# A two-layer trunk: value products of attention in one run, and a last norm applied to token rows

## The chip, the cores and the metric

One NeuronCore of one Trainium2 chip runs the whole kernel. The metric is device microseconds of one execution. Five engines work side by side, each through its own instructions in a fixed order: TensorE (PE; its weight loads are listed as PEld), VectorE (DVE), ScalarE (ACT), GpSimd (POOL) and SyncE (SP, which here only issues DMAs). TensorE reads SBUF and writes PSUM, which has eight banks of 512 fp32 per partition; VectorE and ScalarE read and write both.

## The reference

Two layers over 256 tokens of width 1024, everything in float32. Layer 0 mixes tokens by multi-scale pooling, layer 1 by attention over shared keys and values; each mixer is followed by a causal convolution FFN (inner width 2816) and a gated per-layer embedding, and the whole ends in an RMS norm. What the change touches, cut to its core:

```python
def rmsnorm(x, g):
    return x * lax.rsqrt(jnp.mean(x * x, axis=-1, keepdims=True) + EPS) * g

# attention, 16 heads of 64 in 4 groups; three branches, each a softmax over its keys
o_c = einsum('bghqc,bgcd->bghqd', p_c, vc)          # 15 compressed keys
o_s = einsum('bghqk,bgqkd->bghqd', p_s, vs_g)       # selected blocks
o_w = einsum('bghqk,bgkd->bghqd', p_w, vw)          # window of 512
out = gate0 * o_c + gate1 * o_s + gate2 * o_w

return rmsnorm(x, norm_final)                       # (1, 256, 1024)
```

With 256 tokens the selected blocks and the window are both all causal keys.

## The kernel before, in words

The residual stream `x` lies channel-major in SBUF: 8 tiles (KT) of 128 channels by 256 tokens. A large product is made of three TensorE products of fp32r parts (high times high, high times low, low times high); the parts of weights and activations are split off by ScalarE and VectorE.

**Attention.** Heads are taken two at a time; there are 8 such pairs (`pairs`), numbered n, and the order is written out by hand in `LOOP` (L50): one word is one step, `+1` and `+2` are steps for a later pair, `X` is a slice of filler work (the compressed branch, later the output projection). For a pair the steps are S (scores on PE), M (row maxima, DVE), E (exponentials with sums, ACT), F (factors), W (weighting of the probabilities), T (`turn`: four PE transposes of 128x128 into one PSUM bank, three times, z = 0, 1, 2), P (`parts`: copy of such a bank to SBUF, tile `pt`; z = 0 on ACT, z = 1 and 2 on DVE), V (`values`) and G (`gather`). The written order is not the final one: a planner issues, for each engine, the instruction of highest priority that it takes for ready; the priority is the place in the program, moved forward or back by the entries of `PR` (L60, `lead`).

`values(n, u, z)` (L833) works for two pairs at once, so only for odd n. It multiplies turned probabilities (128 keys by 512 columns) with values (128 keys by 64) into one bank `o`: pair n - 1 (s = 0) goes to PSUM partitions 0 to 63, pair n (s = 1) to 64 to 127, so that each product uses 64 of the 128 columns of the array. z = 0 and 1 are one product of 512 columns per pair, z = 2 is two of 256 columns per pair, z = 3 is the compressed branch (512 columns, tiles `vz` and `pc`). They are fp32, and each product shows as two weight loads and two matmuls in the profile. The order is s = 0, then s = 1 in each z. `V0` and `V1` stand in the middle of the round, `V2` and `V3` near its end, and `V3` has a priority of -20. All have the line of the helper `mm`, L99. `gather` (L900) reads bank `o` when all of it is there (ACT L907, DVE L908) and makes the operand `xo` of the output projection, which is filler work from n = 5 on and, for its last part, follows the loop (`tail`, L957).

**Last norm (L990 to L1016).** For each of the 8 tiles of `x`: ACT squares it (L1001), POOL adds tiles 0 to 5 (L1003), and ACT multiplies the tile by its gain (`scaled`, L996) into `xg`. One-column products on PE sum over partitions: the sum of tiles 0 to 5 first, then tile 6, then the two halves of tile 7. `rstd_of` (DVE L216, POOL L218) makes the factor r per token, with tokens on partitions. As `xg` has its tokens along the free dimension, `row_of` (L257) spreads r to all partitions: two diagonal matrices (DVE L264, ACT L262) and two products with ones. VectorE multiplies `xg` with that row in four steps of 128x512 (L1015), and each step is sent out by a DMA of 256 KB (L1016), from SP and ACT in turn. The host transposes the result.

Of the kernel before, what the change touches and what calls it, by code (L numbers as in the profile page):

```python
# [10 lines left out]
F32 = mybir.dt.float32  # L11
# [3 lines left out]
AF = mybir.ActivationFunctionType  # L15
ALU = mybir.AluOpType
AX = mybir.AxisListType

P = 128
T = 256  # L20
D = 1024
KT = D // P
# [22 lines left out]
BANKS = ((1, 2, 3), (0, 4))  # L45
# [1 line left out]
LEAD = 2  # L47


LOOP = 'W2 S0+2 X S2+1 X W0 X T0 M1+1 T1 M2+1 P0 E2+1 X X X T2 E1+1 P1 V0 M0+2 V1 P2 S1+2 X F+1 E0+2 X W1+1 V2 V3 G X X'  # L50

FILL = (('c0', -2), ('c1', 3), ('o0', 5), ('o1', 7))

# [3 lines left out]

PTS = 8

PR = {'P1': 100, 'W0': 40, 'W2': 100, 'V3': -20, 'w': -20, 'M1': 10}  # L60

PRE = 1

# [15 lines left out]
def body(ctx, tc, xt, xT, pT, pos, colsd, band, wpool, wup, wdn, wgate, wproj, wkv, wq, wqg, wout,  # L79
         cw1, cw2, out):  # L80
    nc = tc.nc
    V, S, E, G = nc.vector, nc.scalar, nc.tensor, nc.gpsimd
    const = ctx.enter_context(tc.tile_pool(name="const", bufs=1))
    wp = ctx.enter_context(tc.tile_pool(name="wp", bufs=3))
    xp = ctx.enter_context(tc.tile_pool(name="xp", bufs=2))
# [4 lines left out]
    def lead(what):  # L90

        n = PR.get(what, 0)
        return tc.high_priority(offset=n) if n else ExitStack()

    def bank(i, shape=(P, 2, T), dt=F32):
        return psum.tile(list(shape), dt, name=f"bank{i}", tag=f"bank{i}")

    def mm(o, w, x, first, last):
        E.matmul(o, w, x, start=first, stop=last, skip_group_check=True)  # L99
# [15 lines left out]
    for layer in range(2):  # L115
        if layer:
            chunks += [(wkv[k], 1) for k in range(KT)]
            n = len(chunks)
# [33 lines left out]
    def take():  # L152
        ahead(1)
        taken[0] += 1
        w = made[taken[0] - 1]
        made[taken[0] - 1] = None
        return w
# [34 lines left out]
    def col(name, i=0, n=1):  # L192
        a = COLS[name][0] + i
        return cols[:, a:a + n]

    ident = col("ident", 0, 128)
# [16 lines left out]
    def rstd_of(ss, name):  # L213
        n = ss.shape[-1]
        m = sm.tile([P, n], F32, name="ms", tag="ms")
        V.tensor_scalar(m, ss, 1.0 / D, EPS, op0=ALU.mult, op1=ALU.add)  # L216
        r = sm.tile([P, n], F32, name=name, tag=name)
        G.tensor_tensor(r, m, mhalf[:, :n], op=ALU.pow)  # L218
        return r
# [13 lines left out]
    b = bank(7, (P, 512))  # L233
# [5 lines left out]
    for i in range(2):  # L239
        ss = sm.tile([P, 1], F32, name=f"ss{i}")  # L240
        S.activation(sqs, xtok[:, i], AF.Square, accum_out=ss)
        r = rstd_of(ss, f"rc{i}")
# [11 lines left out]
        else:  # L254
            S.activation(us[:, k], ub[k], AF.Copy, scale=col("mix0", k))

    def row_of(b, r, both=False):  # L257

        dg = xp.tile([P, 2, P], F32, name="dg", tag="sq", bufs=2)
        for i in range(2):  # L260
            if i and both:
                S.activation(dg[:, i], ident, AF.Copy, scale=r[:, i:i + 1])  # L262
            else:
                V.tensor_scalar(dg[:, i], ident, r[:, i:i + 1], None, op0=ALU.mult)  # L264
        for i in range(2):
            mm(b[:, 256 + i * P:256 + (i + 1) * P], ones, dg[:, i], True, True)
        return b[:, 256:]
# [257 lines left out]
    def attention_layer(ap):  # L525
# [6 lines left out]
        for i in range(2):  # L532
            t = ap.tile([P, 2048], F32, name="w1", tag="big", bufs=2)
            nc.sync.dma_start(t, cw1[i])
            w1.append(t.rearrange("p (i h) -> p i h", i=16))
            t = ap.tile([P, 64], F32, name=f"w2{i}", bufs=1)
# [11 lines left out]
        for k in range(KT):  # L548
            if k == KT - 1:
                rows = finish()  # L550
            w = take()
# [8 lines left out]
        rc, row = rows()  # L560
# [11 lines left out]
        def rope(src, n, w, cc, sc_):  # L572
            sh = ap.tile([P, 512], F32, name="rsh", tag="rsh", bufs=2)
            t = ap.tile([P, 512], F32, name="rt", tag="rt", bufs=1)
            v = lambda a: a[:, :n * w].rearrange("p (n w) -> p n w", n=n)
            if n * w == 512:
                V.stream_shuffle(v(sh), src, SHUF)
            else:
                S.copy(v(t), src)
                V.stream_shuffle(sh[:, :n * w], t[:, :n * w], SHUF)  # L580
            bc = lambda a: a[:, None, :].to_broadcast([P, n, w])
            V.tensor_tensor(v(t), src, bc(cc), op=ALU.mult)
            V.tensor_tensor(v(sh), v(sh), bc(sc_), op=ALU.mult)
            V.tensor_add(t[:, :n * w], t[:, :n * w], sh[:, :n * w])
            return v(t)
# [25 lines left out]
        VV = ap.tile([P, 2, 8, 64], F32, name="vv", bufs=1)  # L611
# [48 lines left out]
        for i in range(2):  # L660
            hb = bank((7, 1)[i], (P, 512))
            o = hb[:, 0:75]
# [6 lines left out]
            h = ap.tile([P, 60], F32, name="gh", tag="gh", bufs=1)  # L669
            V.tensor_scalar(h, o[:, 0:60], bcol, None, op0=ALU.add)  # L670
            t = ap.tile([P, 60], F32, name="gt", tag="gtt", bufs=1)
# [7 lines left out]
            if i == 0:  # L679
                for s in range(2):  # L680
                    mm(hb[s * 64:(s + 1) * 64, 256:286].rearrange("p (a b) -> p a b", a=2), w2[0],
                       gl[:, s::2, :], True, True)
                t = rope(hb[:, 256:286].rearrange("p (a b) -> p a b", a=2), 2, 15, Cc_[:, 0, 0:15],
                         Cc_[:, 1, 0:15])
# [3 lines left out]
            else:  # L688
# [6 lines left out]
                for p in range(2):  # L695
                    o = hb[:, 256 + p * 64:320 + p * 64]
# [3 lines left out]
                VZ = ap.tile([P, 4, 2, 64], F32, name="vz", bufs=1)  # L700
                G.memset(VZ, 0.0)
                for j in range(4):
                    k = slice(32 * j, 32 * j + 32)
# [126 lines left out]
            else:  # L830
                S.copy(t, u["t", z])

        def values(n, u, z):  # L833


            p, s, jj = pairs[n]
            if not s:
                return
            if z == 0:
                u["o"] = bank(BANKS[1][n // 2 % len(BANKS[1])], (P, 512))  # L840
            for t in range(2 if z == 2 else 1):
                for s in range(2):
                    g = 2 * p + s
                    w = U[n - 1 + s]["h", z] if z < 3 else PC[p]
                    v = VV[:, 0, 4 * z + g] if z < 2 else VV[:, 1, 4 * t + g] if z == 2 else VZ[:, 2 * jj + s, p]
                    o = u["o"][64 * s:64 * s + 64]
                    if z == 2:
                        o, w = o[:, T:], w[:, t * T:(t + 1) * T]
                    mm(o, v, w, z == 0, z == 3)


        PC = {}
# [71 lines left out]
        U = {}  # L924
# [18 lines left out]
        for n in range(-LEAD, NPAIR):  # L943
# [6 lines left out]
            if n in FLUSH:  # L950
                filler(100)
            for w in LOOP.split():
                step(w, n)
# [36 lines left out]
    b = bank(2, (P, 512))  # L990
    acc = xp.tile([P, T], F32, name="sqa", tag="sqa", bufs=1)
    xg = xp.tile([P, 2, KT, T], F32, name="xg", tag="xs", bufs=2)
    xg, sq = xg[:, 0], xg[:, 1]

    def scaled(k):
        S.activation(xg[:, k], x[:, k], AF.Copy, scale=col("final", k))  # L996

    for k in range(KT):
        for i in range(2 if k == KT - 1 else 1):
            c = slice(i * P, i * P + P) if k == KT - 1 else slice(0, T)  # L1000
            S.activation((acc if k == 0 else sq[:, k])[:, c], x[:, k, c], AF.Square)  # L1001
        if 0 < k < KT - 2:
            G.tensor_tensor(acc, acc, sq[:, k], op=ALU.add)  # L1003
        if k >= KT - 3:
            for i in range(2):
                mm(b[:, i:i + 1], (acc if k == KT - 3 else sq[:, k])[:, i * P:(i + 1) * P], ones[:, 0:1],
                   k == KT - 3 and i == 0, k == KT - 1)
        if k < KT - 2:
            scaled(k)
    for k in range(KT - 2, KT):  # L1010
        scaled(k)
    row = row_of(b, rstd_of(b[:, 0:2], "rcol"), True)
    for m in range(4):
        sl = slice(2 * m, 2 * m + 2)
        V.tensor_tensor(xg[:, sl], xg[:, sl], row[:, None, :].to_broadcast([P, 2, T]), op=ALU.mult)  # L1015
        (nc.sync, nc.scalar)[m % 2].dma_start(out[:, sl], xg[:, sl])  # L1016


def _constants():
# [93 lines left out]
```

## Time and profile before

| | |
|---|---|
| time, median of 3 runs | 635.78 us (635.47 to 637.28) |
| the profiled execution | 632.52 us |
| its span, first to last instruction | 630.7 us |
| PE busy | 609.0 us (97%) |
| DVE, ACT, POOL busy | 536.2, 403.7, 45.1 us |
| mean granted TensorE clock | 0.992 |
| attention loop, value products and their fillers | about 320 to 396 us of the span |
| last norm | about 616 to 630.7 us |

A span is divided into stretches with different limits, and so the share of busy time of the whole is only a first look. A matmul's record reaches over the filling and draining of the array, so records overlap; how long a group of matmuls holds the array is read from its start to the start of the next matmul.

### The profile page before, as it was taken

How to read it: one execution, taken by the hardware profiler on the slowest of the kernel's cores; microseconds unless marked ns; L12 is line 12 of the kernel's file. 1: busy time of each engine (PE TensorE's matmuls, PEld its weight loads, DVE VectorE, ACT ScalarE, POOL GpSimd, SP SyncE). 2: the span in 40 equal slices, each digit the busy share in tenths (PEclk: the TensorE clock that was granted, in tenths of full speed). 3: DMA queues.
4: the chain of work that ended last, by engine and by line, in shares of the span. 5: the costliest groups of instructions: out<-in, count | busy, mean ns of one | idle time of the engine just before them, and what ended most of it. 6: DMA issues, size and time to landing. Idle time of an engine off the chain costs nothing. (4 is left out here: it accounts for less than half of the span.)

```text
span 630.7 us, 10850 instructions
## 1 busy us (share of the span) xinstructions
PE 609.0 (97%) x4122; PEld 544.7 (86%) x4122; DVE 536.2 (85%) x984; ACT 403.7 (64%) x776; POOL 45.1 (7%) x69
## 2 busy tenths in 40 slices
PE   8999999999999999999889999999999999999994
PEld 7789999999999999999855666789999999999994
DVE  3999999999988889476998865799999998888854
ACT  4868766666676767373686641696566667666642
POOL 1510000000000323000000000300000000000321
PEclk9999999999999999999989999999999999999997
DMA  8775467655553146755541111346765454552002
GB/s 336 292 258 201 182 218 266 235 204 178 176 184 145 51 151 235 288 201 157 181 103 68 68 67 68 118 167 235 255 229 190 172 175 184 198 201 101 2 2 67
DMA packets 24261, 107.32 MB, mean 170 GB/s; under 512 B 3601, under 2 KB 7697, under 8 KB 15889
## 3 DMA queue, kind: packets, MB, share of 16 engines
q1 hardware_dynamic: 23776, 105.58, 47.2%
q10 hardware_dynamic: 432, 1.05, 0.5%
q8 instruction: 32, 0.52, 0.3%
q14 instruction: 21, 0.16, 0.1%
HBM read 101.80 MB, written 1.05 MB: 163 GB/s over the span
## 5 line engine op out<-in xcount | busy, mean ns | idle before, releaser
L99 PE MATMUL bank<-xs,wh 128*128 128x512 f32 (+1 forms) x960 | 295.4, 365 | 0.4 <-DVE xs L228 0.2
L99 PE MATMUL bank<-xs,wl 128*128 128x256 f32 x832 | 233.6, 281 | 0.6 <-DVE wl L149 0.6
L99 PEld LDWEIGHTS bank<-xs,wh 128*128 128x128 f32 x960 | 171.8, 189 | 30.2 <-DVE xs L228 3.1
L149 DVE TENSOR_TENSOR wl<-raw,wh 128x1024 fp32r<-128x1024 f32 (+2 forms) x142 | 166.6, 1184 | 20.4 <-ACT wh L147 20.4
L147 ACT CAST wh<-raw 128x1024 fp32r<-128x1024 f32 (+2 forms) x144 | 141.6, 1006 | 36.2 <-PE bank L99 27.8
L99 PEld LDWEIGHTS bank<-xs,wl 128*128 128x128 f32 x832 | 157.5, 189 | 1.3 <-DVE wl L149 1.3
L99 PE MATMUL bank<-al,dh 128*128 128x256 f32 x352 | 99.3, 283 | 0.0
L99 PE MATMUL bank<-ah,dl 128*128 128x256 f32 x352 | 99.1, 283 | 0.0
L99 PE MATMUL bank<-ah,dh 128*128 128x256 f32 x352 | 98.4, 284 | 0.3
L99 PEld LDWEIGHTS bank<-ah,dh 128*128 128x128 f32 x352 | 66.4, 190 | 2.3 <-ACT ah L389 0.7
L99 PEld LDWEIGHTS bank<-al,dh 128*128 128x128 f32 x352 | 67.4, 191 | 0.0
L99 PEld LDWEIGHTS bank<-ah,dl 128*128 128x128 f32 x352 | 67.2, 191 | 0.0
L380 ACT ACTIVATE t<-un,cols 128x256 f32<-128x256 f32 x88 | 52.4, 601 | 10.0 <-DVE un L376 9.8
L166 ACT CAST dh<-draw 128x1024 fp32r<-128x1024 f32 x44 | 46.2, 1052 | 19.1 <-PE bank L99 16.0
L374 ACT COPY ub<-bank 128x256 f32<-128x256 f32 x88 | 32.0, 367 | 40.9 <-PE bank L99 40.8
L279 POOL TENSOR_TENSOR sqa<-sqa,sq 128x256 f32<-128x256 f32 x35 | 29.6, 846 | 393.3 <-issue 369.6
L167 DVE TENSOR_TENSOR dl<-draw,dh 128x1024 fp32r<-128x1024 f32 x44 | 53.6, 1218 | 0.0
L381 DVE SCALAR_TENSOR_TENSOR t<-un,cols,t 128x256 f32<-128x256 f32 x88 | 42.0, 481 | 5.4 <-ACT t L380 5.1
L382 DVE SCALAR_TENSOR_TENSOR t<-un,cols,t 128x256 f32<-128x256 f32 x88 | 42.0, 482 | 1.6
L375 DVE TENSOR_TENSOR ub<-bank,ub 128x256 f32<-128x256 f32 x88 | 36.5, 419 | 0.5
L376 DVE TENSOR_TENSOR un<-ub,rrow 128x256 f32<-128x256 f32 x88 | 36.6, 419 | 0.1
L99 PE MATMUL bank<-qs,wh 128*128 128x256 f32 x144 | 28.6, 294 | 0.0
(194 smaller groups left out, 847.2 us busy)
## 6 DMA issues: line engine op xcount, KB each, us to landing
raw<-in_wup SPq DMA_DIRECT2D x44, 1024.0 KB, 4.8
draw<-in_wdn SPq DMA_DIRECT2D x44, 512.0 KB, 4.9
raw<-in_wgate SPq DMA_DIRECT2D x8, 1024.0 KB, 4.8
raw<-in_wkv SPq DMA_DIRECT2D x8, 768.0 KB, 4.4
raw<-in_wq SPq DMA_DIRECT2D x4, 1024.0 KB, 5.1
raw<-in_wout SPq DMA_DIRECT2D x4, 1024.0 KB, 5.0
raw<-in_wproj SPq DMA_DIRECT2D x2, 1024.0 KB, 4.9
w<-in_cw SPq DMA_DIRECT2D x2, 1024.0 KB, 6.8
```

Source lines behind the costliest of these rows:

```text
L99: E.matmul(o, w, x, start=first, stop=last, skip_group_check=True)
L147: S.copy(hi[:, sl], raw[:, sl])
L149: e.tensor_tensor(lo[:, sl], raw[:, sl], hi[:, sl].bitcast(F32), op=ALU.subtract)
L166: S.copy(hi, raw)
L167: V.tensor_sub(lo, raw, hi.bitcast(F32))
L279: G.tensor_tensor(acc, acc, t, op=ALU.add)
L374: S.copy(ub, up[i][h][:, 1])
L375: V.tensor_tensor(ub, up[i][h][:, 0], ub, op=ALU.add)
L376: V.tensor_tensor(un[:, h, 2:], ub, row, op=ALU.mult)
L380: S.activation(t1, un[:, h, 2:], AF.Identity, scale=c[2], bias=c[3])
L381: V.scalar_tensor_tensor(t1, un[:, h, 1:T + 1], c[1], t1, op0=ALU.mult, op1=ALU.add)
L382: V.scalar_tensor_tensor(t1, un[:, h, 0:T], c[0], t1, op0=ALU.mult, op1=ALU.add)
```

## The change

The value products of two pairs are issued in one step `V`, at the end of the round, with a priority of +60 instead of four steps; inside, z runs 2, 0, 1, 3 and s runs 1, 0. The last norm no longer spreads r over a row. 16 PE transposes of 128x128 bring the scaled tiles token-major into four PSUM banks, those of tiles 0 to 5 in the program behind the one-column products of tile 6 and ahead of those of tile 7, those of tiles 6 and 7 behind these. VectorE (tokens 0 to 127) and ScalarE (tokens 128 to 255) multiply each bank by r, now a factor per partition, into `o`. Three DMAs go out: 256 KB twice from SP, and 512 KB from ACT. The output's shape is (P, 2, D) and the host no longer transposes.

```diff
-LOOP = 'W2 S0+2 X S2+1 X W0 X T0 M1+1 T1 M2+1 P0 E2+1 X X X T2 E1+1 P1 V0 M0+2 V1 P2 S1+2 X F+1 E0+2 X W1+1 V2 V3 G X X'
+LOOP = 'W2 S0+2 X S2+1 X W0 X T0 M1+1 T1 M2+1 P0 E2+1 X X X T2 E1+1 P1 M0+2 P2 S1+2 X F+1 E0+2 X W1+1 V G X X'
-PR = {'P1': 100, 'W0': 40, 'W2': 100, 'V3': -20, 'w': -20, 'M1': 10}
+PR = {'P1': 100, 'W0': 40, 'W2': 100, 'V': 60, 'w': -20, 'M1': 10}
...
-        def values(n, u, z):
+        def values(n, u):
...
-            if z == 0:
-                u["o"] = bank(BANKS[1][n // 2 % len(BANKS[1])], (P, 512))
-            for t in range(2 if z == 2 else 1):
-                for s in range(2):
-                    g = 2 * p + s
...
-                    mm(o, v, w, z == 0, z == 3)
+            u["o"] = bank(BANKS[1][n // 2 % len(BANKS[1])], (P, 512))
+            for z in (2, 0, 1, 3):
+                for t in range(2 if z == 2 else 1):
+                    for s in (1, 0):
+                        g = 2 * p + s
...
+                        mm(o, v, w, z == 2 and t == 0, z == 3)
...
+    tb = [[bank(4, (P, 512)), bank(5, (P, 512))], [bank(6, (P, 512)), bank(7, (P, 512))]]
+    def turned(k):
+        for i in range(2):
+            E.transpose(tb[k // 4][i][:, k % 4 * P:(k % 4 + 1) * P], xg[:, k, i * P:(i + 1) * P], ident)
...
         if k < KT - 2:
             scaled(k)
+        if k == KT - 2:
+            for j in range(KT - 2):
+                turned(j)
     for k in range(KT - 2, KT):
         scaled(k)
-    row = row_of(b, rstd_of(b[:, 0:2], "rcol"), True)
-    for m in range(4):
-        sl = slice(2 * m, 2 * m + 2)
-        V.tensor_tensor(xg[:, sl], xg[:, sl], row[:, None, :].to_broadcast([P, 2, T]), op=ALU.mult)
-        (nc.sync, nc.scalar)[m % 2].dma_start(out[:, sl], xg[:, sl])
+        turned(k)
+    r = rstd_of(b[:, 0:2], "rcol")
+    o = xp.tile([P, 2, D], F32, name="o", tag="xs", bufs=2)
+    for g in range(2):
+        sl = slice(512 * g, 512 * g + 512)
+        V.tensor_scalar(o[:, 0, sl], tb[g][0], r[:, 0:1], None, op0=ALU.mult)
+        nc.sync.dma_start(out[:, 0, sl], o[:, 0, sl])
+        S.activation(o[:, 1, sl], tb[g][1], AF.Copy, scale=r[:, 1:2])
+    nc.scalar.dma_start(out[:, 1], o[:, 1])
```

`row_of` loses its argument `both`, which only the last norm used.

## Rows read from the trace of the kernel before

**Rows 1.** The page, part 1: busy us, share of the span, instructions.

```profile
PE 609.0 (97%) x4122; PEld 544.7 (86%) x4122; DVE 536.2 (85%) x984; ACT 403.7 (64%) x776; POOL 45.1 (7%) x69
```

**Rows 2.** Stretches: length, busy us of PE, PEld, DVE, ACT, POOL; clock, DMA.

```profile
310.00:320.00 10.00, 8.06 (x42) 5.66 (x40) 10.00 (x21) 7.16 (x28) 0.00 (x0) 0.84 0.69 206
320.00:330.00 10.00, 7.33 (x42) 4.62 (x40) 9.80 (x27) 8.67 (x32) 0.00 (x0) 0.98 0.44 104
330.00:356.00 26.00, 24.62 (x140) 14.30 (x140) 21.52 (x60) 15.63 (x60) 0.00 (x0) 1.00 0.21 75
356.00:396.00 40.00, 38.32 (x244) 26.94 (x243) 26.02 (x50) 15.65 (x46) 0.17 (x3) 1.00 0.16 58
```

**Rows 3.** Timeline of PE, first round of value products: start, us, matmuls, idle before.

```profile
324.20 1.07 PE L99 MATMUL bank<-pt,vv 128*64 128x512 f32 x2
325.20 0.74 PE L99 MATMUL bank<-kk,qq 128*128 128x512 f32 x2
...
332.23 1.93 PE L99 MATMUL bank<-pt,vv 128*64 128x512 f32 x8
334.09 0.50 PE L99 MATMUL bank<-kk,qq 128*128 128x512 f32 x1
334.52 1.08 PE L99 MATMUL bank<-pt,vv 128*64 128x256 f32 x6
335.53 0.74 PE L99 MATMUL bank<-kk,qq 128*128 128x256 f32 x4
...
336.54 1.08 PE L99 MATMUL bank<-pc,vz 128*64 128x512 f32 x4
337.55 0.74 PE L99 MATMUL bank<-kk,qq 128*128 128x512 f32 x2
```

**Rows 4.** Timeline of PE, the last round of value products.

```profile
385.52 1.08 PE L99 MATMUL bank<-pt,vv 128*64 128x512 f32 x4
...
395.58 1.11 PE L99 MATMUL bank<-xo,wh 128*128 128x256 f32 x5 [0.68 <-ACT xo L907]
```

**Rows 5.** Stretches: all matmuls on `vv` first, on `vz` second.

```profile
356.00:396.00 40.00, 8.39 (x32) 2.35 (x32) 0.00 (x0) 1.00 0.16 58
...
356.00:396.00 40.00, 4.29 (x8) 0.76 (x8) 0.00 (x0) 1.00 0.16 58
```

**Rows 6.** Groups of instructions by line: the copies of `parts` on VectorE.

```profile
L829 DVE COPY pt<-bank 128x512 f32<-128x512 f32 x16 | 10.9, 685 | 1.4 <-PE bank L823 1.4
```

**Rows 7.** Timeline of PE ahead of the fall of the granted clock.

```profile
314.57 0.74 PE L99 MATMUL bank<-kk,qq 128*128 128x256 f32 x4 [1.83 <-ACT pe L785]
```

**Rows 8.** Timeline of all engines in the last norm.

```profile
620.55 0.53 PEld L99 LDWEIGHTS bank<-ones,xg 128*128 128x128 f32 x4
...
621.56 0.52 PEld L99 LDWEIGHTS bank<-ones,xg 128*128 128x128 f32 x4 [0.49 <-ACT xg L1001]
...
622.45 0.70 POOL L218 TENSOR_TENSOR rcol<-ms,mhalf 128x2 f32<-128x2 f32 x1 [4.06 <-DVE ms L216]
623.18 0.29 DVE L264 TENSOR_SCALAR dg<-cols,rcol 128x128 f32<-128x128 f32 x1 [0.81 <-POOL rcol L218]
```

**Rows 9.** One line's instructions: duration ns min/median/max, first and last start.

```profile
L613 ACT ACTIVATE vv<-bank,rcol x2: 688/695/702, 273.7 to 275.5; 128x512 f32<-128x512 f32 x2
...
L1016 SPq DMA_DIRECT2D out<-xg x2: 338/342/347, 625.0 to 626.2; - x2
L1016 ACTq DMA_DIRECT2D out<-xg x2: 338/341/344, 625.7 to 626.8; - x2
DMA to landing us min/median/max: 2.4/2.8/3.1
```

**Rows 10.** Stretch in which the output's bytes move.

```profile
625.70:629.30 3.60, 0.00 (x0) 0.00 (x0) 1.07 (x2) 0.00 (x0) 0.00 (x0) 0.50 0.89 291
```

**Rows 11.** Timeline: eight transposes of `turn`, with PE's next matmul.

```profile
338.39 1.09 PE L823 MATMUL bank<-cols,pe 128*128 128x128 f32 x8
339.24 0.60 PE L99 MATMUL bank<-kc,qq 128*128 128x32 f32 x4
```

More of the change, by code (lines that the diff above doesn't have):

```diff
@@ L255, in body, with row_of @@
             S.activation(us[:, k], ub[k], AF.Copy, scale=col("mix0", k))
-    def row_of(b, r, both=False):
+    def row_of(b, r):
         dg = xp.tile([P, 2, P], F32, name="dg", tag="sq", bufs=2)
         for i in range(2):
[L261 to L264, printed above, removed]
+            V.tensor_scalar(dg[:, i], ident, r[:, i:i + 1], None, op0=ALU.mult)
         for i in range(2):
@@ L838, in values @@
                 return
-            if z == 0:
-                u["o"] = bank(BANKS[1][n // 2 % len(BANKS[1])], (P, 512))
-            for t in range(2 if z == 2 else 1):
-                for s in range(2):
-                    g = 2 * p + s
[L844 to L848, printed above, removed]
-                    mm(o, v, w, z == 0, z == 3)
+            u["o"] = bank(BANKS[1][n // 2 % len(BANKS[1])], (P, 512))
[3 more added lines that the diff above has]
+                        g = 2 * p + s
+                        w = U[n - 1 + s]["h", z] if z < 3 else PC[p]
+                        v = VV[:, 0, 4 * z + g] if z < 2 else VV[:, 1, 4 * t + g] if z == 2 else VZ[:, 2 * jj + s, p]
+                        o = u["o"][64 * s:64 * s + 64]
+                        if z == 2:
+                            o, w = o[:, T:], w[:, t * T:(t + 1) * T]
+                        mm(o, v, w, z == 2 and t == 0, z == 3)
         PC = {}
@@ L1106 @@
            for k, v in arrays.items()]
-    o = nc.dram_tensor("out_0", (P, KT, T), F32, kind="ExternalOutput").ap()
+    o = nc.dram_tensor("out_0", (P, 2, D), F32, kind="ExternalOutput").ap()
     with tile.TileContext(nc) as tc, ExitStack() as ctx:
@@ L1111 @@
     y = np.asarray(r.results[0]["out_0"])
-    return con(y.transpose(1, 0, 2).reshape(D, T).T).reshape(1, T, D)
+    return con(y.transpose(1, 0, 2)).reshape(1, T, D)
```

## The prediction

> **What bounds the kernel now.** I read the page's busy part first: PE is busy for 97% of the span, VectorE for 85% [rows 1]. That does not say that time taken from PE is time won, so the second view is the table of stretches [rows 2]. It shows two kinds of attention. From 356 us on PE holds 38.32 of 40 us while VectorE needs 26.02 and ScalarE 15.65: PE is the limit, and the X steps give it projection products for its gaps. Before 356 us the two run level: VectorE 9.80 of 10 us in 320 to 330, where PE has 7.33, and 21.52 of 26 us in 330 to 356, where PE has 24.62. There a shorter PE helps only where PE itself is the last to be ready.
>
> The third view is PE's timeline, for how long a value product holds the array, from its start to the next matmul's start [rows 3]. Two records at 324.20 (V0 of the even pair alone, half of the array's columns) hold it for 1.00 us and show as 1.07. Four records in the last round, both halves side by side, show as 1.08 [rows 4]. The second half of the columns costs nothing if it is issued next to the first. In the kernel before it often is not: the planner issues V0 of the even pair as soon as its operand is ready, the rest comes eight microseconds later, out of step, with scores or projection products between.
>
> **The value products.** The eight records at 332.23 hold the array for 1.86 us, two paired products; one pair costs 1.00, so a further pair in the same run costs 0.86. A round after the change has 10 products: V2 (two pairs of 256 columns, together one pair of 512), V0, V1 and V3, so 1.00 + 3 x 0.86 = 3.58 us. The first round before costs 1.00 + 1.86 + 1.01 + 1.01 = 4.88 us [rows 3].
>
> Rounds 3 and 4, in the stretch where PE is the limit, have 8.39 + 4.29 = 12.68 us of records [rows 5]. They stand in ten separate groups, each reaching 0.07 over the next start as at 324.20, and in one of them products of z = 2 and z = 3 lie side by side and are counted twice for 0.6: 12.68 - 0.7 - 0.6 = 11.4 us. After: 2 x 3.58 = 7.16. Gain 4.2 us, all of it on PE and, by rows 2, on the path.
>
> In the last round there is one more item. At 395.58 PE waits 0.68 us for `gather`'s copy [rows 4], because projection products have been spent between the value products. With V at +60 these products are left over to cover that copy. I count 0.68. What could eat it is the opposite wait: the whole run now begins with the product that needs the last copy of the round, 0.685 us on VectorE [rows 6]. In rounds 3 and 4 projection products lie under it, so nothing; without that cover up to 1 us a round (transposes' drain and copy), 2 us.
>
> In rounds 1 and 2 there is no projection work yet. What can be won are the groups inside the PE-limited part: the first round's 1.86 + 1.01 + 1.01 = 3.88 against 3.58, so 0.30. The early half at 324.20 wins nothing, since PE waits soon after it anyway (7.33 busy of 10) [rows 2, 3]. The second round looks like the first, somewhat more broken; at most 0.8. So +1.1 us at best. At worst PE stands idle for the drain and the copy ahead of each run, 1.05 us twice, with nothing to do, and gets back 0: -2.1 us. And behind the run, which is ahead of the next scores by priority, scores wait up to 3.58 us; VectorE, ScalarE and `gather` wait with them. They have a lead of two pairs, so I price that at nothing here and make it a rival. I take -0.3 us, near the middle, as the trace shows both signs.
>
> Attention: 4.2 + 0.68 - 0.3 = 4.6 us, with ends of 4.9 + 1.1 = 6.0 and 4.2 - 2 - 2.1 = 0.1.
>
> **The last norm.** Before, from the factor r at 623.16, the chain is the two diagonals (VectorE and ScalarE begin at 623.18), the products with ones, four products on VectorE, and DMAs issued from 625.0 to 626.8, the last landing 2.4 us later at 629.2 [rows 8, 9]. After, diagonals and products with ones are gone. VectorE does two steps of 512 from PSUM; the nearest rows are its copies from a bank, 0.685 [rows 6]. ScalarE does two of 512 from PSUM with a factor per partition, 0.70 [rows 9]. Counted from the same r: first DMA at 623.18 + 0.69 + 0.1 = 623.97, the last two (SP's second, ACT's only) at 623.18 + 2 x 0.69 + 0.1 = 624.66. That is 1.0 us earlier for the first and 2.1 for the last.
>
> Against it stand the 12 transposes of tiles 0 to 5. In PE's order they come after the one-column products of tile 6, whose weight loads end at 621.08, and ahead of those of tile 7, which before began at 621.56 [rows 8]. A transpose costs (339.24 - 338.39) / 8 = 0.11 us in a row [rows 11], 12 of them 1.3 us: PE is free for tile 7 at 622.4 instead of 621.56. The four last transposes run under the mean and the power on POOL (0.70) and cost nothing. The products of tile 7 lose some waiting for ScalarE's second half that they had, so r is later by 0.7 to 0.8. If the planner puts the transposes ahead of that point, into gaps, r is not late at all.
>
> Then the transfer. The output is 1.05 MB, which moved at 291 GB/s over 3.6 us [rows 10]. All of it is now issued within 0.7 us, so the end is set by the first issue plus that transfer. With r late by 0.75, the first DMA goes at 624.7, 0.3 before; if the same rate holds, the gain is 0.3. But the 3.6 us before held waits for VectorE (issues spread over 1.8 us), and the last quarter landed 2.4 us after its issue; with 512 KB in the last DMA instead of 256, 0.9 us more at 291 GB/s, the end is 625.4 + 2.4 + 0.9 = 628.7, a gain of 0.5. I take 0.5 us. Best: no delay of r and the second reckoning, 1.25 and up to 1.7 if the rate is better than 291. Worst: each transpose by the length of a whole record between separate ones, 0.27 (1.09 for eight, less seven steps of 0.117), 3.3 us, so r 2.7 us late and a loss of 1.5.
>
> The Trainium skill speaks for that worst end: "TensorE: Matmul & The Clock Gate", Part 4: PE-mode transpose, gives about 275 ns for a 128x128 transpose within a kernel. By that figure 12 of them would be an estimated 3.3 us and the norm would lose 1.5 us instead of winning 0.5. The trace does not agree for transposes in a row: 96 of them run through `turn`, and eight hold PE for 0.85 us [rows 11]; I go by the row.
>
> **Sum.** 4.6 + 0.5 = 5.1 us. The profiled execution took 632.52 us (span 630.7), so one like it would take 627.4. The median of the timed runs is 635.78, 3.3 us above the profiled one; the saved work is the same in both, so the forecast is 635.78 - 5.1 = 630.7 us. Nothing behind attention takes the gain back: the FFN's stretches are PE-limited, as the 97% of the whole says [rows 1], and the DMA share in 330 to 396 is 0.16 to 0.21 [rows 2], so weights are not late.
>
> **Rivals.** (a) The round is limited by the chain from scores to copies also after 356 us, and half of the 4.9 us turns into waits for VectorE and ScalarE: 4.9/2 - 0.3 + 0.5 = 2.6, 633.2 us. For it: VectorE still has 26 of 40 us and every wait of PE there is for a copy or an exponential. Against it: projection products can fill.
>
> (b) The change does not do what it says. The planner decides by its own idea of readiness, and the products come apart again, as they did before. Then the rounds cost what they cost now, and only the norm counts: 635.3 us. For it: the two products of V3 stand together in the program and still came apart in rounds 3 and 4 (4.29 us for eight records, four times the 1.07 of a lone half [rows 3, 5]), at a priority of -20. Against it: the first product of the new order needs the newest operand, and +60 is ahead of the fillers.
>
> (c) Slower: the run starves the pipeline. It holds PE for 3.58 us at a stretch ahead of the scores of the next pairs, where before scores went between the groups (334.09 and 335.53) [rows 3]. In rounds 1 to 3 scores are still to be made. If VectorE and ScalarE have no stock, each loses 3.58 less the 1.4 us that a group boundary took so far, 2.2 a round, 6.5 in three. PE's idle time can then bring down its clock: after a wait of 1.83 us [rows 7] the granted clock of 310 to 320 was 0.84 [rows 2], 3.2 us at 1.2 instead of 2.4 GHz, so 1.6 us of work time. The early half product at 324.20 fills just such a thin stretch, and it goes. Two such falls cost up to 3.2. Loss 6.5 + some of 3.2, say 8, against a gain of 5.1: 638.7 us. It decides from 1.7 us of starvation a round on. Against it: the lead of two pairs.
>
> (d) Transposes by the long price: 2 us less gain, 632.7 us. The trace is against it.
>
> **How the numbers follow.** Forecast 0.60 (its own range 628.3 to 632.3), (a) 0.15, (b) 0.11, (c) 0.11, (d) 0.03. 0.3% is 1.9 us, about what a measurement of this kernel can tell from no change. Faster: forecast, (a) mostly and (d), 0.75. Same: most of (b) and the edge of (a), 0.13. Slower: (c) and a little of (b), 0.12. The range for 8 in 10 takes in the best ends (6.0 + 1.3, so 628.5, and a little for the spread of the medians) and (a) and reaches to the edge of (b): 627.9 to 635.0.
>
> **What would show it.** In the profile after: in each of four rounds one run of value products, 3.6 us from start to next start, with no other matmul inside; no two-record group eight microseconds ahead. The stretch from 356 us to the end of attention shorter by 4 to 5 us, PE without the 0.68 us wait before `xo`. In the norm: 12 transposes between the one-column products of tiles 6 and 7, the power on POOL 0.7 us later against the end of the gate products, and three DMAs within 0.8 us. The prediction is wrong if value products come apart, if PE waits more than 1 us ahead of each run, or if the clock falls in 324 to 345 us.

## The result, and the profile after

The changed kernel takes 627.86 us (median of 4 runs, 626.25 to 630.54), the kernel before 635.62 beside it: a ratio of 0.9887, interval 0.9862 to 0.9912. Run twice more as an anchor for the experiments it gave 629.21 us both times, at ratios of 0.9929 (0.9909 to 0.9950) and 0.9919 (0.9894 to 0.9944). So it is faster by 4.5 to 7 us, by the two longer comparisons about 5. The forecast was 5.1 us less, 630.7 us; the first median lies at the lower edge of the forecast's range, 627.9 to 635.0, the two anchors well inside. The profiled execution of after took 630.54 us (span 628.8), the slowest of its four.

The busy part of the page hardly moves, as an average over stages does [rows 1]:

```profile
PE 606.5 (96%) x4134; PEld 550.7 (88%) x4134; DVE 535.1 (85%) x981; ACT 405.7 (65%) x777; POOL 47.7 (8%) x69
```

The same four stretches as in [rows 2] (length, busy us of PE, PEld, DVE, ACT, POOL, then the granted clock, DMA share, GB/s):

```profile
310.00:320.00 10.00, 8.12 (x41) 5.97 (x39) 9.44 (x19) 6.88 (x28) 0.00 (x0) 0.76 0.69 205
320.00:330.00 10.00, 7.79 (x37) 6.41 (x35) 8.54 (x21) 7.64 (x27) 0.00 (x0) 0.67 0.27 65
330.00:356.00 26.00, 24.41 (x142) 16.33 (x142) 23.22 (x66) 17.28 (x66) 0.00 (x0) 0.89 0.17 57
356.00:396.00 40.00, 38.83 (x284) 31.45 (x283) 28.27 (x54) 18.66 (x50) 0.17 (x3) 1.00 0.30 113
```

Two things are to be seen. From 356 us on PE is still the limit, with 284 matmuls in the stretch where 244 were. And the granted clock is 0.76, 0.67 and 0.89 before that, where it was 0.84, 0.98 and 1.00.

The value products, on PE's timeline (start, length, matmuls, idle before), in the first, second and last round; they answer to [rows 3, 4]:

```profile
337.98 2.80 PE L99 MATMUL bank<-pt,vv 128*64 128x256 f32 x16
340.61 1.03 PE L99 MATMUL bank<-pc,vz 128*64 128x512 f32 x4
341.57 0.74 PE L99 MATMUL bank<-kk,qq 128*128 128x256 f32 x4
...
350.82 2.80 PE L99 MATMUL bank<-pt,vv 128*64 128x256 f32 x16 [0.74 <-DVE pt L826]
353.45 1.03 PE L99 MATMUL bank<-pc,vz 128*64 128x512 f32 x4
354.41 0.66 PE L892 MATMUL bank<-cols,spread 128*128 128x128 f32 x4
...
385.27 2.80 PE L99 MATMUL bank<-pt,vv 128*64 128x256 f32 x16
387.90 1.03 PE L99 MATMUL bank<-pc,vz 128*64 128x512 f32 x4
388.86 0.50 PE L99 MATMUL bank<-xo,wh 128*128 128x256 f32 x2
```

In each round 20 records stand together with no other matmul among them, and the run holds the array for 341.57 - 337.98 = 3.59 us. PE waits 0.74 us ahead of one run. Behind the last run it goes on with no wait, where it had waited 0.68 us for `gather` [rows 4].

The last norm, on the timeline of all engines, from the last gate product on; it answers to [rows 8]:

```profile
619.04 0.28 PE L99 MATMUL bank<-ph,wl 128*128 128x256 f32 x1
...
619.96 1.51 PE L1000 MATMUL bank<-cols,xg 128*128 128x128 f32 x12
...
621.20 0.53 PEld L99 LDWEIGHTS bank<-ones,xg 128*128 128x128 f32 x4
...
622.09 0.70 POOL L218 TENSOR_TENSOR rcol<-ms,mhalf 128x2 f32<-128x2 f32 x1 [4.76 <-DVE ms L216]
622.82 1.27 ACT L1026 ACTIVATE o<-bank,rcol 128x512 f32<-128x512 f32 x2 [1.77 <-POOL rcol L218]
622.82 1.41 DVE L1024 TENSOR_SCALAR o<-bank,rcol 128x512 f32<-128x512 f32 x2 [0.81 <-POOL rcol L218]
```

Twelve transposes stand ahead of the weight loads of tile 7 (621.20). The time from the start of the last gate product to the start of the power on POOL, 2.35 us before (620.10 to 622.45), is now 3.05.

The output's DMAs (durations, first and last start) and the stretch in which its bytes move, against [rows 9, 10]:

```profile
L1025 SPq DMA_DIRECT2D out<-o x2: 338/342/347, 623.6 to 624.3; - x2
...
L1027 ACTq DMA_DIRECT2D out<-o x1: 344/344/344, 624.1 to 624.1; - x1
...
624.30:627.20 2.90, 0.00 (x0) 0.00 (x0) 0.00 (x0) 0.00 (x0) 0.00 (x0) 0.76 0.96 362
```

Three issues within 0.7 us; the bytes move at 362 GB/s, where they had moved at 291.

**A reckoning by place.** One execution of a kernel differs from the next by up to 5 us, so a part of the change is better read between two marks of the trace than from the total. The marks are the starts of matmuls: the first score product, the first matmul behind the second round of value products (R2), the first product of layer 1's FFN, its first down product, the last gate product, and the end of the span. The last column is the mean granted clock between the first two marks. Between the down product and the last gate product all kernels here agree within 0.6 us.

| us, profiled executions | scores to R2 | R2 to FFN | FFN to down | last gate to end | clock, scores to R2 |
|---|---|---|---|---|---|
| before | 44.53 | 47.64 | 19.73 | 10.63 | 0.96 |
| after | 44.96 | 43.39 | 22.55 | 9.71 | 0.81 |
| after, first anchor | 42.24 | 43.38 | 21.84 | 9.69 | 0.92 |
| after, second anchor | 43.52 | 43.41 | 21.29 | 9.70 | 0.88 |
| values alone | 44.96 | 43.39 | 21.08 | 10.62 | 0.81 |
| norm alone | 45.01 | 47.64 | 19.68 | 9.74 | 0.96 |
| halves in turn | 47.56 | 46.93 | 21.62 | 9.69 | 0.89 |
| four steps, newest first | 41.84 | 45.42 | 19.55 | 11.14 | 0.92 |
| four steps and norm | 44.75 | 45.33 | 19.55 | 9.71 | 0.81 |
| four steps, norm, four buffers | 42.10 | 45.31 | 19.55 | 9.71 | 0.92 |
| split first | 41.87 | 43.39 | 21.99 | 9.72 | 0.92 |
| four buffers | 41.94 | 43.40 | 22.01 | 9.71 | 0.92 |
| transposes last | 43.78 | 43.37 | 21.12 | 9.64 | 0.88 |
| dummies | 44.73 | 43.38 | 21.42 | 9.71 | 0.96 |

So the change wins 4.25 us in the PE-limited rounds in every profiled execution, between -0.4 and +2.3 in rounds 1 and 2, 0.92 in the norm, and loses 1.4 to 2.8 at the start of the FFN (values alone counted with it). For the profiled pair: -0.43 + 4.25 - 2.82 + 0.92 = 1.92 of the 1.98 by which the spans differ (630.73 and 628.75). That pair understates the change: before's was one of its fastest executions (632.52 us, of 632.3 to 637.3), after's the slowest of four. Some of the spread of totals lies ahead of the change, though not for this pair: in seven of the fourteen profiled executions the granted clock is 0.79 in 6 to 14 us and the first score product comes at 311.0 to 311.2 us; in the others, before and after among them, it is 1.00 and 309.4 to 309.7 us.

### The profile page after: what moved, and what is told of

Same layout as the page of the kernel before. It is cut to its first block, busy times and chain, and to the rows that moved or that the text cites. A ratio compares the mean times of both kernels' runs of the same rounds, so it can differ in the third digit from the quotient of the medians.

```text
span 628.8 us, 10871 instructions
## 1 busy us (share of the span) xinstructions
PE 606.5 (96%) x4134; PEld 550.7 (88%) x4134; DVE 535.1 (85%) x981; ACT 405.7 (65%) x777; POOL 47.7 (8%) x69
## 4 chain that ended last, share of the span: by engine, by line
PE 82%; DVE 4%; ACT 3%; issue 2%; DMA 1%; SPq 1%; POOL 1%; POOLq 0%; DVEq 0%; ACTq 0%
PE bank L99 80%; PE bank L820 2%; ACT wh L147 1%; DMA draw<-in_wdn 1%; DVE wl L149 1%; POOL sqa L276 0%; DVE dl L167 0%; DVE pt L826 0%; SPq L592 0%; ACT pe L782 0%; DMA kk<-kp 0%; DVE nm L770 0%; SPq L701 0%; ACT xs L227 0%; DVE x L739 0%
## 5 line engine op out<-in xcount | busy, mean ns | idle before, releaser
L276 POOL TENSOR_TENSOR sqa<-sqa,sq 128x256 f32<-128x256 f32 x35 | 31.3, 895 | 397.0 <-issue 370.3
L386 ACT CAST ah<-sg 128x256 fp32r<-128x256 f32 x44 | 17.8, 404 | 17.3 <-DVE sg L383 17.3
```

The costliest lines, as they stand in the source:

```text
L276: G.tensor_tensor(acc, acc, t, op=ALU.add)
```

## The experiments

The kernel before ran beside each of the three groups of experiments: 634.75, 634.33 and 634.72 us.

**Each part alone.** Values alone keeps the old norm; norm alone keeps the old four steps.

```diff
 values alone, from the kernel after
-        turned(k)
...
+    row = row_of(b, rstd_of(b[:, 0:2], "rcol"), True)
 norm alone, from the kernel after
-PR = {'P1': 100, 'W0': 40, 'W2': 100, 'V': 60, 'w': -20, 'M1': 10}
+PR = {'P1': 100, 'W0': 40, 'W2': 100, 'V3': -20, 'w': -20, 'M1': 10}
```

> The value products in one run as in the change; the last norm as before. Theory A (the idle half of the array's columns is the cause): the four runs hold the array for 3.6 us each, the end of attention is some 4 us earlier or more, and 6.0 to 7.0 of the 7.8 us are here: 628.6 to 629.6 us against 635.6. Theory B (the norm is worth more than its 0.8 us in the traces): less than 5 us here, above 630.6. Theory C (the medians differ by the clock that the executions happened to get): a gain of about the 1.9 us by which the two profiled spans differ, 633 to 634 us.

> The last norm as in the change; the value products as before. Theory A: from the end of the gate products to the end of the span the changed trace is 0.84 us shorter, so 634.8 us, within the noise of no change. Theory B: 2 us or more, below 633.6. The prediction's step had 0.5.

Measured: values 630.39 us, ratio 0.9933 (0.9912 to 0.9955); norm 633.67, ratio 0.9985 (0.9969 to 1.0001). The two make 4.4 and 1.1 us, 5.4 together, about the whole change. Values alone stays below the 6 to 7 us of theory A: that expectation was made from the 7.8 us by which the first medians differ, more than the anchors showed later. The norm by itself can't be told from nothing by its time; its place in the table shows it: 9.69 to 9.74 in every profile with this norm (9.64 with its transposes moved), 10.62 to 11.14 with the old.

**Halves in turn.** The kernel after, one run still, but all products of one pair first and then all of the other, so that the two halves of the array's columns are no longer issued side by side.

```diff
-            for z in (2, 0, 1, 3):
-                for t in range(2 if z == 2 else 1):
-                    for s in (1, 0):
+            for s in (1, 0):
+                for z in (2, 0, 1, 3):
+                    for t in range(2 if z == 2 else 1):
```

> The changed kernel, but inside a run the five products of the odd pair come first and then the five of the even pair, so that two halves of the columns never work side by side; place, priority and contiguity of the run are kept. Theory A: a product alone takes 0.86 us, eight of the 512 kind 6.9 us and 0.14 to start, so a run takes about 7.0 instead of 3.6 us, and four runs 13.7 us more: where PE is the limit (rounds 3 and 4) 6.8 us, in all 634 to 641 us. Rival (what helps is that the run is whole and early, not that halves are paired): same as the changed kernel, 627.9, within 1.5 us.

Measured: 636.61 us, ratio 1.0023 (1.0005 to 1.0040), 7.4 above the 629.21 of the anchors, which ran in other groups; by the ratios 6 to 6.6 us. PE's timeline in the first round:

```profile
338.72 2.86 PE L99 MATMUL bank<-pt,vv 128*64 128x256 f32 x12
341.36 0.59 PE L99 MATMUL bank<-pc,vz 128*64 128x512 f32 x1
341.42 0.59 PE L99 MATMUL bank<-pt,vv 128*64 128x512 f32 x1
341.78 0.59 PE L99 MATMUL bank<-pc,vz 128*64 128x512 f32 x1
341.85 1.45 PE L99 MATMUL bank<-pt,vv 128*64 128x512 f32 x3
343.13 1.02 PE L99 MATMUL bank<-pc,vz 128*64 128x512 f32 x2
344.08 0.72 PE L99 MATMUL bank<-kk,qq 128*128 128x256 f32 x4
```

The run holds the array for 5.36 us and not 3.59, 1.77 more, though not the 7.0 expected. The rows show why: the first pair's last products (`vz` at 341.36 and 341.78) stand among the second pair's (`vv`), and the single records have the second pair begin at 340.50, 1.78 us behind the first. So each pair still works beside the other for about half of its 3.58 us, and only the other half is paid for. From R2 to the FFN there are two runs, and the table has 46.93 - 43.39 = 3.54 us more, twice 1.77. Four runs would make 7.1 us, about what the total shows, but in rounds 1 and 2 the place itself varies too much to tell. That is the cause shown, in rounds 3 and 4: it is the two halves side by side that win the time. One run without them wins nothing.

**Pairs side by side without the run.** The kernel before, with the four steps V0 to V3 where they were; only the order inside a step is turned, so that the half whose operand is newest is issued first.

```diff
-                for s in range(2):
+                for s in (1, 0):
```

> The kernel before with one edit: in each of the four value steps the odd pair's product comes first, so that the even pair's can't run ahead alone; places and priorities stay. Theory A: a round costs 4 x 1.0 = 4.0 us or a little less instead of 4.9 to 5.9, in the PE-limited rounds 3 and 4 3.3 us less in all, 1 us short of the single run's gain: 630 to 632.5 us. Rival (one whole run with high priority is what helps): no change, 635.6 within 1.5 us.

Measured: 629.54 us, ratio 0.9924 (0.9907 to 0.9940), for one changed expression. PE's timeline:

```profile
363.58 1.94 PE L99 MATMUL bank<-pt,vv 128*64 128x512 f32 x8
...
370.18 1.07 PE L99 MATMUL bank<-pc,vz 128*64 128x512 f32 x2
...
371.50 1.07 PE L99 MATMUL bank<-pc,vz 128*64 128x512 f32 x2
...
390.04 1.03 PE L99 MATMUL bank<-pc,vz 128*64 128x512 f32 x4
...
391.75 1.11 PE L99 MATMUL bank<-xo,wh 128*128 128x256 f32 x5 [0.69 <-ACT xo L907]
```

Most pairs now stand together (x8, x4), V3 of the third round still comes apart (370.18 and 371.50), and the wait for `gather` stays. So from R2 to the FFN it wins 2.2 us where the one run wins 4.25. But it loses nothing at the start of the FFN (19.55), and ends level. With the new norm added:

> The kernel before with the two halves in the order s = 1, s = 0 in its four steps V0 to V3, and with the new last norm. Theory: the gains stand in places that don't touch, so they add: four steps in that order 4.8 us and the norm 1.0 us, ratio about 0.991, 628.5 to 629 us; first FFN product to first down product 19.6 us, gate products to end of span 9.7 us. Rival: the one run is worth more than pairs side by side, because it also leaves the projection for later; then this is slower than the changed kernel by 1 us or more.

628.94 us, ratio 0.9918 (0.9895 to 0.9942), beside 629.21 and 0.9919 for the kernel after, run next to it. The sum is the same; the 2 us that the run wins beyond this are lost again at the start of the FFN. Neither beats the other.

**The clock.** The kernel after, with 26 dummy products (128x512, bf16, low priority) added in the first four passes of the loop (they run from 312.5 to 324.8 us, ahead of the first value products), so that PE is less idle there; the output is not touched.

```diff
+            if n < 2:
+                busy(5 if n < 0 else 8)
```

> The changed kernel with 26 products of 128x512 bf16 into a bank that nobody reads, 0.21 us each, at low priority, in the thin stretches ahead of the first value products (5, 5, 8 and 8 in the first four rounds); output unchanged. If falls of the clock take back part of the gain (half speed at 315.2 to 325.4 and 328.8 to 335.7 us in the trace, 17 us), the clock stays up there, the spread of the executions shrinks, and the median is 2 to 4 us below the changed kernel's. Rival (VectorE and ScalarE bound the first rounds, the clock of PE is hidden there): no gain, and up to 3 us of loss where the extra products stand in the way.

Measured: 631.32 us, ratio 0.9955 (0.9938 to 0.9971), against 629.21 for the kernel after, run next to it:

> The changed kernel itself, so that the others of this call have it on the same chip. If the clock that an execution gets is behind part of the result, its executions spread over 4 us again (626.3 to 630.5 so far), the longer ones with the lower mean clock; the median should lie between 627.5 and 629.5, that is before less 4.4 (values alone) less 1.1 (norm alone), and up to 1.5 more if the two help each other.

The first three stretches of the run with dummies, and on PE's timeline its longest wait there:

```profile
310.00:320.00 10.00, 9.11 (x54) 5.88 (x53) 8.68 (x17) 5.84 (x27) 0.00 (x0) 1.00 0.70 205
320.00:330.00 10.00, 7.21 (x50) 5.19 (x48) 9.79 (x25) 8.36 (x26) 0.00 (x0) 1.00 0.28 67
330.00:356.00 26.00, 23.07 (x142) 15.77 (x143) 23.16 (x65) 17.61 (x69) 0.00 (x0) 0.93 0.17 56
```
```profile
329.02 0.72 PE L99 MATMUL bank<-kk,qq 128*128 128x256 f32 x4 [2.77 <-DVE f L796]
```

The clock stays at 1.00 until 330 us (0.93 behind it), and still R2 comes 44.73 us after the first score product, as late as in the profiled execution of after with its falls (44.96). VectorE has 9.79 of 10 us, and PE waits 2.77 us for it. So holding the clock up this way gains nothing. It does not settle what the falls cost: the dummies also stand in PE's order and may have moved VectorE's work.

The table says more on that. Seven profiles have the attention of after and no dummies (after, its anchors, values alone, split first, four buffers, transposes last), and they come in three levels: with a mean clock of 0.92 from scores to R2 that stretch takes 41.87 to 42.24 us, with 0.88 it takes 43.52 and 43.78, with 0.81 it takes 44.96 twice. The kernels of four steps in the new order follow the same line (0.92: 41.84 and 42.10; 0.81: 44.75); the run with dummies, 44.73 at 0.96, lies off it. Both kernels with the old value products have 0.96, and over all timed executions the mean clock of the whole was 0.986 to 0.996 for norm alone and 0.981 to 0.985 for values alone. So the new attention runs these rounds at a lower clock than the old, and more of it goes with up to 3 us of later R2. That the falls are the cause is not shown, as no run changed the clock alone.

**What makes the start of the FFN slower.** Three lines of the kernel after's timeline, and three of its DVE rows there:

```profile
400.50 0.42 ACT L275 ACTIVATE sq<-x 128x256 f32<-128x256 f32 x1 [1.60 <-POOL sqa L276]
...
403.31 0.50 PE L99 MATMUL bank<-xs,wh 128*128 128x512 f32 x1 [1.17 <-DVE xs L228]
...
405.85 0.50 PE L99 MATMUL bank<-xs,wh 128*128 128x512 f32 x1 [1.57 <-DVE xs L228]
```
```profile
398.66 1.21 DVE L149 TENSOR_TENSOR wl<-raw,wh 128x1024 fp32r<-128x1024 f32 x1
...
402.24 1.01 DVE L228 SCALAR_TENSOR_TENSOR xs<-x,cols,xs 128x256 fp32r<-128x256 f32 x1 [1.49 <-ACT xs L227]
403.18 1.75 DVE L167 TENSOR_TENSOR dl<-draw,dh 128x1024 fp32r<-128x1024 f32 x1
```

ScalarE stands behind POOL's sums of squares, VectorE behind ScalarE, PE behind VectorE's splits `xs`. Two kernels try to take that out. The first gives the splits a higher priority (an entry `'x': 10` in `PR`, used here):

```diff
-            dosplit(k)
+            with lead("x" if layer else ""): dosplit(k)
```

> The changed kernel with ScalarE's splits of x (xs) ahead of its squares at the start of layer 1's FFN, by a priority of +10. In the trace of the changed kernel PE waits there 1.17 and 1.57 us for xs, since a square ahead of it in ScalarE's queue waits for a buffer that POOL still reads; attention ends 3.9 us earlier than before, but the gate products only 1.1. If that wait takes the gain back: 1 to 2.5 us below the changed kernel. Rival (POOL's additions of the squares bound this place, as the row factor needs them): within 0.5 us of the changed kernel, because the wait for r takes the place of the wait for xs.

Measured: 628.31 us, ratio 0.9924 (0.9899 to 0.9949), 21.99 us from FFN to down; by its ratio it can't be told from the first anchor (0.9929), and the place is no shorter. The wait moved: PE now stands 2.25 us ahead of the norm's one-column products, for POOL:

```profile
406.11 0.61 PE L99 MATMUL bank<-ones,sqa 128*128 128x1 f32 x4 [2.25 <-POOL sqa L276]
```

The second gives the squares four buffers (`wide` is 1 in layer 1's FFN alone):

```diff
-                t = xp.tile([P, T], F32, name="sq", tag="sq", bufs=2)
+                t = (fpool[0] if wide else xp).tile([P, T], F32, name="sq", tag="t1" if wide else "sq", bufs=4 if wide else 2)
```

> The changed kernel, with four buffers for the squares of the norm at the start of layer 1's FFN (they take the place of a tile not yet in use there) instead of two. Theory: in the changed kernel ScalarE has issued a square ahead of the splits that PE waits for, and stands 1.60 us until POOL's addition gives its buffer back; with four buffers it goes on. First FFN product to first down product: 19.6 to 20.8 us in place of 21.8 to 22.6, no wait of ScalarE for `sqa`, PE without the waits of 1.2 and 1.6 us for `xs`; time 1 to 2.5 us below the changed kernel, about 627.3. Rival: POOL's seven additions (7.2 to 8.4 us, the factor waits for the last) set the end of this place whatever ScalarE does; 21.8 to 22.6 us as before, and the time of the changed kernel, 629 within 1 us.

> The changed kernel itself, as an anchor for the three runs beside it: about 629 us, ratio 0.99 to 0.993; first FFN product to first down product 21.8 to 22.6 us.

Measured: 628.54 us, ratio 0.9916 (0.9888 to 0.9943), 22.01 us. My theory fell. ScalarE's waits for POOL are gone but for 0.28 us, and PE still waits 1.58 us for `xs`, as in the first anchor (1.57):

```profile
396.42 1.76 DVE L149 TENSOR_TENSOR wl<-raw,wh 128x1024 fp32r<-128x1024 f32 x1
398.10 1.84 DVE L228 SCALAR_TENSOR_TENSOR xs<-x,cols,xs 128x256 fp32r<-128x256 f32 x2
399.87 1.75 DVE L167 TENSOR_TENSOR dl<-draw,dh 128x1024 fp32r<-128x1024 f32 x1
401.54 1.83 DVE L228 SCALAR_TENSOR_TENSOR xs<-x,cols,xs 128x256 fp32r<-128x256 f32 x2
```
```profile
402.55 0.50 PE L99 MATMUL bank<-xs,wh 128*128 128x512 f32 x1 [1.58 <-DVE xs L228]
```

VectorE works without a break, and its order has two splits of weights (1.76 and 1.75 us) among those of `x`. In the kernel before it made seven splits of `x` in a row there, 5.38 us from 402.85. So what holds PE up is VectorE's order at this seam, which ScalarE's waits only hid. That order as the cause is read from the rows; a kernel with the weights' splits behind was not run.

The clock adds to it. Behind PE's waits it fell in some executions; the same stretch (columns as in the table of stretches above) in after and in values alone:

```profile
406.00:410.00 4.00, 4.00 (x18) 3.48 (x19) 3.41 (x6) 3.09 (x6) 2.00 (x2) 0.67 0.35 128
```
```profile
406.00:410.00 4.00, 3.64 (x24) 3.06 (x23) 3.41 (x8) 3.13 (x5) 1.61 (x1) 1.00 0.40 115
```

With a fall (after, the first anchor, four buffers) the place takes 22.55, 21.84 and 22.01 us; at 1.00 throughout (the second anchor, values alone, transposes last, dummies) 21.29, 21.08, 21.12 and 21.42. PE's idle time in the place splits the loss. It is 0.67 us before and, in the order named, 2.74, 1.76 and 1.76 with a fall, 2.30, 2.10, 2.12 and 2.29 without. Without a fall the added idle time is the whole loss (1.4 to 1.6 us of idle time, 1.4 to 1.7 us of length); with a fall it is 1.1 to 2.1 us, and another 0.75 to 1.2 us come on top that the waits don't explain.

The buffers put on the kernel of four steps, which doesn't have the problem:

> As the run of four steps and the new norm, with four buffers for the squares at the start of layer 1's FFN as well. Theory: with four steps ScalarE waits only 0.18 us for POOL there, so the buffers bring nothing: within 0.7 us of that run, and this pair of runs shows what the comparison can tell. Rival: the buffers free ScalarE at a place of their own, whatever the order of attention, and it is faster by 1 us or more.

628.82 us, ratio 0.9918 (0.9896 to 0.9939), 0.12 from its neighbour; 19.55 us from FFN to down in both.

**Transposes last.** The kernel after, with all 16 transposes behind the one-column products in the program.

```diff
-        if k == KT - 2:
-            for j in range(KT - 2):
-                turned(j)
...
+    for k in range(KT):
         turned(k)
```

> The changed kernel with the 12 transposes of tiles 0 to 5 moved behind the one-column products of tile 7. If they make the factor r late, as the prediction says and the trace shows (tile 7's products start at 621.20, right behind the transposes, against 620.5 when its squares are there), r comes 0.7 us earlier and the whole is 0.6 to 0.8 us shorter than the changed kernel. Rival: the end is set by the output's transfer, whose bytes need 3 us after the first issue whatever r does earlier; then the first issue moves by the same 0.7 and so does the end, unless the transposes now last longer than POOL's power: no gain, or a loss of up to 0.5.

Measured: 627.95 us, ratio 0.9908 (0.9887 to 0.9930). It didn't do what it was made for. The planner moved ten transposes ahead again, as PE was free:

```profile
619.00 1.29 PE L1000 MATMUL bank<-cols,xg 128*128 128x128 f32 x10
...
620.12 0.28 PE L99 MATMUL bank<-ones,xg 128*128 128x1 f32 x2
...
621.08 0.70 POOL L218 TENSOR_TENSOR rcol<-ms,mhalf 128x2 f32<-128x2 f32 x1 [4.71 <-DVE ms L216]
```

The power starts 3.01 us after the last gate product, in place of 3.05. The 1.3 us between its median and the first anchor's are thus not from this place, and the intervals of the two overlap.

## Why the prediction was right, and where it was not

**The run of value products: right.** Predicted 3.58 us, whole in each round; measured 3.59. Halves in turn shows that the reason given, the second half of the columns at no cost when it is issued next to the first, is the cause.

**Rounds 3 and 4: right, a little large.** Predicted 4.2 + 0.68 = 4.9; measured 47.64 - 43.39 = 4.25. The products came as counted: the value products of the two rounds held the array for 11.41 us before, from each group's start to PE's next matmul, and 7.18 after, 4.23 less. What failed is the 0.68 us on top. The wait for `gather` is gone, but PE's idle time from R2 to the FFN fell only from 1.68 to 1.46 us: the waits of 0.68 us for `gather` and 0.68 for a copy of `pt` went, and two of 0.35 behind VectorE's additions to `x` and 0.29 for the FFN's `xs` came (before, then after):

```profile
384.93 0.66 PE L823 MATMUL bank<-cols,pe 128*128 128x128 f32 x4 [0.68 <-ACT pt L831]
```
```profile
384.36 0.51 PE L99 MATMUL bank<-xo,wh 128*128 128x256 f32 x2 [0.35 <-DVE x L739]
```

**Rounds 1 and 2: the price within its ends on one side only.** Taken -0.3, with ends of +1.1 and -2.1. The profiled execution of after has -0.4; the anchors +1.0 and +2.3. The best end was too low. On average the seven profiles with this attention take 43.32 us there, against 44.77 for the two with the old, so +1.45 in place of -0.3.

**"Nothing behind attention takes the gain back": wrong.** This is the step that failed. I argued from PE's 97% over the whole span [rows 1], the very average that the first lines of the prediction warn of, and didn't read the first 10 us of the FFN. There PE follows VectorE's splits, and 1.4 to 2.8 us of the gain are given back, on average 1.9 over the five profiles with the run and this place unchanged (after, its anchors, values alone, transposes last). The larger gains of rounds 1 and 2 and of the norm made up for it. By these averages the terms are 4.25 + 1.45 - 1.9 + 0.9 = 4.7 us, where the prediction added 4.9 - 0.3 + 0 + 0.5 = 5.1. So the sum came out right partly by luck, because errors were of opposite sign.

**The norm: the delay right, the end too small.** r is 0.70 us later against the last gate product; 0.7 to 0.8 was predicted. For the price of a transpose the row was right: 12 in 1.51 us with the last one's tail, their weight loads in 1.38, and from start to start 0.11 us each. The Trainium skill ("TensorE: Matmul & The Clock Gate", Part 4: PE-mode transpose) gives about 275 ns within a kernel. The trace agrees with that as the length of one record (0.27 us), not as the price of a transpose in a row. The gain of 0.5 became 0.92, and with it the rate was not 291 but 362 GB/s: the first issue came 0.39 us earlier against the last gate product, near the 0.3 predicted, and the bytes then moved in 2.9 us instead of 3.6. That the old stretch of [rows 10] held waits for VectorE, as the prediction suspected, fits with this; no run tested it by itself.

**The rivals.** (a) Half the gain of rounds 3 and 4 in new waits: no, 4.25 of 4.9 came. (b) Products apart again: no, but halves in turn shows its price, and more than that. (c) Starvation: half of it came. VectorE and ScalarE did not starve, as R2 is on average earlier and not 2.2 us a round later. But the clock did fall, in the stretch that I had named as a sign of a wrong prediction, and more than without the change: from scores to R2 its mean is 0.81 to 0.92, and 0.96 in both kernels with the old value products, where norm alone has its fall in 320 to 330 us (0.83) and before in 310 to 320 [rows 2]. The kernel is faster all the same, so as a sign it was badly chosen. (d) No.

**The basis.** Putting the profiled execution's savings on the median was sound; all three medians of after lie 1.5 to 2.8 us below the forecast, where the medians of before beside them lie 0.2 to 1.5 us below the 635.78 that the sum started from.

## What to carry to other kernels

Where two instructions can share a unit, issue first the one whose operand comes last: its sibling is then ready, and the pair mostly stays together even under a planner (here one pair of a round still came apart). When a stretch gets shorter, read the order of every engine at the next seam, for the average of the span does not show what waits there. And compare edits between fixed marks in the trace: here R2 to the FFN agrees to 0.1 us among profiles of the same attention, where totals differ by up to 5; scores to R2 and FFN to down, where the granted clock falls, differ by 3 and 1.5 us, and there one pair of profiles settles nothing.

## What was not expected of the hardware

VectorE and POOL hold each other up. POOL's additions of 128x256 at the start of the FFN take 0.80 us, and up to 2.2 where VectorE splits weights beside them (durations ns min/median/max; after, then four steps, where no weights' split falls into the row of splits):

```profile
L276 POOL TENSOR_TENSOR sqa<-sqa,sq x7: 725/801/2197, 398.3 to 405.6; 128x256 f32<-128x256 f32 x7
```
```profile
L279 POOL TENSOR_TENSOR sqa<-sqa,sq x7: 736/803/919, 397.3 to 402.6; 128x256 f32<-128x256 f32 x7
```

And VectorE's split of weights takes 1.21 us alone and 1.76 beside POOL in the run with four buffers, its split of `x` 0.48 and 0.95. The Trainium skill ("SBUF — State Buffer", section "SBUF: two separate sides") says that the two share one pair of ports, held by one of them for a whole instruction, when a VectorE instruction has two inputs in SBUF and GpSimd's reads SBUF as well. The longest addition agrees, as it takes about its own time and that of the split of weights beside it (2.2 against 0.80 + 1.21). The others grow by less: the splits by 0.55 and 0.47 us, not by a whole addition of 0.80.
